# Weight sums of a Strassen step by accumulating DMAs inside SBUF, with the block products in another order

## The chip, the cores and the metric

The kernel runs on one core of one Trainium2 chip. The metric is device time in microseconds (us). The engines are PE (TensorE, matrix products), DVE (VectorE), ACT (ScalarE), POOL (GpSimd) and SP (SyncE, which here only issues DMAs). Each engine works through its own list of instructions in order and waits on semaphores for the others. SBUF is the on-chip memory, 128 partitions; PSUM holds the accumulators of matrix products.

## The reference

The kernel computes a trunk of four pre-norm layers over 256 tokens of width 1024, in fp32. Each layer is a mixer with a memory attention beside it, an output projection, and a dense SwiGLU FFN. The change lies in the FFN alone:

```python
def _swiglu(x, w_in, w_out):
    gu = x @ w_in
    return (jax.nn.silu(gu[..., :D_FF]) * gu[..., D_FF:]) @ w_out
```

`D_FF` is 2816, so `w_in` is 1024 x 5632 and `w_out` 2816 x 1024.

## The kernel before, in words

Weights come from HBM in chunks of 512 KB, [128, 2, 512] in fp32: SP issues the load (L124 in `wchunk`, L220 in `strassen`) into one of eight buffers of the pool `wraw`. A product in fp32 precision is made of three matmuls in the faster format fp32r. For that each chunk is split into a high and a low part in `wparts`: ACT casts `whi` (L131), DVE subtracts to get `wlo` (L132). There are eight buffers of `whi` and eight of `wlo`, so a cast waits until PE is through with the chunk eight places ahead. PE then runs hi x hi, hi x lo, lo x hi (L136 to L138; L214 to L216 in `strassen`).

An FFN has six blocks of hidden columns, b = 0 to 5. In blocks 1 and 4, and once in the middle of the output projection (`hidden_products`), a 2 x 2 block product [tokens] x [weights] is made with seven block products in place of eight (Strassen's scheme in Winograd's form). This is `strassen`; I call its three places in a layer A (b = 1), B (b = 4) and C (in the output projection). Four layers make twelve calls.

In such a call the weight quarters are b11, b12 (upper row), b21, b22 (lower row). Each is loaded in two halves of depth, s = 0 and 1, each one chunk of 512 KB. The numbers of the products and the weights that they take are:

| product | weight operand |
|---|---|
| 1 | b11 |
| 5 | t = b11 + b12 |
| 7 | b12 + b22, written over b12 |
| 6 | t + b22, written over t |
| 2 | b21 |
| 4 | t + b21, written over t again |
| 3 | b22 |

The tile t is `wsum` in the profile and sits in a `wraw` buffer too. I write 6_0 for the half of product 6 with s = 0. A half of a product is six matmuls of 128 x 512. Before the change all sums are made by DVE in `plus` (L224), four for each s: eight a call. Products add up in shared accumulators (`banks`): 1 and 2 in one, 5 and 3 in one, 7 and 4 in one, 6 in its own. Between them DVE reads accumulators out: u = acc6 + v, y = acc7 + u (L224), then `out` hands quarters of the result on (`gated`, L905 to L913 for A and B; `quarter`, L936 for C). So product 4 may start in the accumulator of 7 only when y has been read from it, and product 3 in that of 5 only when L911 (in C: L936) has read it.

The order on each engine is set by a scheduler from the order of the code and the dependencies; within an engine it is fixed. n0, n1, ... are the weight chunks that follow a call. `flush` runs work that was put off with `later`, such as the transposes of hidden columns (`hidden`, L890 to L894). In block 4 `hidden_side` makes the token sums that C needs out of such a transposed tile, `src`. `rstd` (L329, L330) and two small products for `lamt` (L694) are POOL's only work near the calls.

Of the kernel before, what the change touches and what calls it, by code (L numbers as in the profile page):

```python
# [13 lines left out]
ALU = mybir.AluOpType  # L14
# [3 lines left out]
P = 128  # L18
# [22 lines left out]
def trunk_kernel(ctx, tc, x, mem, vecs, w_in, w_kv, w_o, w_f1, w_f2, lams, g_final, out):  # L41
    nc = tc.nc
# [85 lines left out]
    def wparts(raw, nk=2, ncol=512):  # L128
        hi = wsplit.tile([P, nk, ncol], F32R, name="whi", tag="whi")
        lo = wsplit.tile([P, nk, ncol], F32R, name="wlo", tag="wlo")  # L130
        nc.scalar.copy(hi, raw)  # L131
        wlast[:] = [nc.vector.tensor_tensor(lo, raw, hi.bitcast(F32), ALU.subtract)]  # L132
        return hi, lo
# [12 lines left out]
    def flush():  # L146
        for item in pend:
            item[0] -= 1
        for item in [i for i in pend if i[0] <= 0]:
            pend.remove(item)  # L150
            item[1]()
# [45 lines left out]
    def strassen(left, right, ab, out):  # L197

        acc = {}
        banks = {1: 1, 2: 1, 5: 5, 3: 5, 7: 7, 4: 7, 6: 6}

        def product(p, w, s):
            b = banks[p]
            if b not in acc:
                acc[b] = ps_acc.tile([P, 512], F32, name="acc", tag="ps")
            lh, ll = ab[p]  # L210
            for k in range(2):
                kc = 2 * s + k
                start, stop = kc == 0 and p == b, kc == 3
                nc.tensor.matmul(acc[b], lh[:, kc, :], w[0][:, k, :], start=start, stop=False, skip_group_check=True)  # L214
                nc.tensor.matmul(acc[b], lh[:, kc, :], w[1][:, k, :], start=False, stop=False, skip_group_check=True)  # L215
                nc.tensor.matmul(acc[b], ll[:, kc, :], w[0][:, k, :], start=False, stop=stop, skip_group_check=True)  # L216

        def load(cols, r):
            raw = wraw.tile([P, 2, 512], F32, name="raw", tag="raw")
            nc.sync.dma_start(raw, cols[r:r + 2 * P, :].rearrange("(c p) n -> p c n", p=P))  # L220
            return raw

        def plus(out, a, b):
            nc.vector.tensor_tensor(out, a, b, ALU.add)  # L224

        part = lambda name: work.tile([P, 512], F32, name=name, tag="att", bufs=NATT)
        b22, sums = [], []
        v, u, y = part("sv"), part("su"), part("sy")
        for s in range(2):
            b11, b12 = (load(c, 2 * s * P) for c in (left, right))  # L230
            b22.append(load(right, 512 + 2 * s * P))
            product(1, wparts(b11), s)
            t = wraw.tile([P, 2, 512], F32, name="wsum", tag="raw")
            plus(t, b11, b12)
            if s == 1:
                nc.scalar.copy(v, acc[1])
            product(5, wparts(t), s)
            flush()
            plus(b12, b12, b22[s])
            product(7, wparts(b12), s)  # L240
            plus(t, t, b22[s])
            product(6, wparts(t), s)
            flush()
            sums.append(t)
        plus(u, acc[6], v)
        plus(y, acc[7], u)
        b21 = [load(left, 512 + 2 * s * P) for s in range(2)]
        for s in range(2):
            product(2, wparts(b21[s]), s)
        out(0, 0, acc[1], None)  # L250
        out(1, 1, acc[5], y)
        flush()
        for s in range(2):
            plus(sums[s], sums[s], b21[s])
            product(4, wparts(sums[s]), s)
            if s == 1:
                out(1, 0, acc[7], u)
            product(3, wparts(b22[s]), s)
            flush()
        out(0, 1, acc[5], u)  # L260

    def negative(rs):
        out = []
# [5 lines left out]
    def token_parts(src):  # L269
        hi = work.tile([P, 4, P], F32R, name="sh", tag="att", bufs=NATT)  # L270
        lo = work.tile([P, 4, P], F32R, name="sl", tag="att", bufs=NATT)
        nc.scalar.copy(hi, src)
        nc.vector.tensor_tensor(lo, src, hi.bitcast(F32), ALU.subtract)
        return hi, lo
# [432 lines left out]
    for i in range(DEPTH):  # L707
# [136 lines left out]
        hab, hsum = {}, {}  # L844

        def hidden_side(k, t, src):

            tt, stt = nc.vector.tensor_tensor, nc.vector.scalar_tensor_tensor
            if k == 0 and t == 0:
                both = big.tile([P, 2, 4, P], F32, name="hsum", tag="big")  # L850
                hsum["d"], hsum["a21"] = both[:, 0], both[:, 1]
                nc.scalar.copy(hsum["d"], src)
            elif k == 0:
                nc.scalar.copy(hsum["a21"], src)
                tt(hsum["d"], hsum["d"], src, ALU.subtract)
                hab[7] = token_parts(hsum["d"])
            elif t == 1:
                tt(hsum["a21"], src, hsum["a21"], ALU.subtract)
                hab[5] = token_parts(hsum["a21"])
                stt(hsum["d"], hsum["d"], -1.0, src, ALU.mult, ALU.subtract)  # L860
                hab[6] = token_parts(hsum["d"])
            else:
                stt(hsum["a21"], src, -1.0, hsum["d"], ALU.mult, ALU.subtract)
                hab[3] = token_parts(hsum["a21"])
                for p, g, t in ((1, 3, 0), (2, 4, 0), (4, 4, 1)):
                    hab[p] = tuple(x[:, :, t * P:(t + 1) * P] for x in hts[g])

        for b in range(6):
# [18 lines left out]
            def hidden(t, s, hh, hl, n, b):  # L887
                tr = ps_x.tile([P, 4, P], F32, name="tr", tag="ps")
                for c in range(n // P):
                    nc.tensor.transpose(tr[:, c, :], s[:, c * P:(c + 1) * P], ident)  # L890
                src = tr[:, :n // P, :]
                hi = hh[:, :, t * P:(t + 1) * P]
                nc.scalar.copy(hi, src)
                nc.vector.tensor_tensor(hl[:, :, t * P:(t + 1) * P], src, hi.bitcast(F32), ALU.subtract)  # L894
                if b in (3, 4):
                    hidden_side(b - 3, t, src)
# [3 lines left out]
            if b in (1, 4):  # L900
                def gated(t, side, ps, add, sg=sg, hh=hh, hl=hl, b=b, up={}):
                    if side == 0:
                        src = ps
                        if add is not None:
                            nc.vector.tensor_tensor(sg[t], ps, add, ALU.add)  # L905
                            src = sg[t]
                        nc.scalar.activation(sg[t], src, AF.Silu, scale=rx[t])
                        up[t, 0] = sg[t]
                    else:
                        up[t, 1] = add if t == 1 else work.tile([P, 512], F32, name="sx", tag="att", bufs=NATT)  # L910
                        nc.vector.tensor_tensor(up[t, 1], ps, add, ALU.add)  # L911
                    if (t, 0) in up and (t, 1) in up:
                        nc.vector.scalar_tensor_tensor(sg[t], up[t, 1], rneg[t], sg[t], ALU.mult, ALU.mult)  # L913
                        later(2, lambda: hidden(t, sg[t], hh, hl, 512, b))

                strassen(gcols, ucols, ab, gated)
            elif n == 512:
                proj([gcols], xT, lambda t, ps: h_out(t, ps, None))
                if b == 0:
                    ab, rneg = tokens_side(xg, xT), negative(rx)  # L920
                proj([ucols], xT, lambda t, ps: h_out(t, None, ps))
            else:
                proj([gcols, ucols], xT, lambda t, ps: h_out(t, ps[:, :n], ps[:, n:2 * n]))
# [14 lines left out]
        def hidden_products():  # L938
            w = w_f2[i, 12 * P:20 * P, :]
            strassen(w[:, :512], w[:, 512:], hab, quarter)  # L940
# [35 lines left out]
```

## Time and profile before

| what | value |
|---|---|
| median of three runs | 1271.62 us (1271.61 to 1271.62) |
| the profiled execution | 1271.41 us, span 1269.7 us |
| granted TensorE clock, mean | 0.999 |
| PE busy | 1258.3 us (99%) |
| DVE busy | 1022.4 us (81%) |
| ACT busy | 753.3 us (59%) |
| POOL busy | 55.7 us (4%) |
| bytes moved by DMA | 227.35 MB, mean 179 GB/s |

How to read it: a row of the groups gives line, engine, operation, output <- inputs, shape and count, then busy time in us and the mean of one in ns, then the idle time of the engine ahead of these instructions and what ended it. A row of the waits gives who waited for what: us in total, times, longest. A row of a timeline gives start and duration in us; matmuls are pipelined, so that their durations overlap and the distance of two starts tells the rate. A row of a stretch gives its length, busy time and count of each engine, the granted clock, the share of the DMA engines, and GB/s.

### The profile page before, as it was taken

To read this page: it belongs to the slowest core of one execution; us is meant where nothing else is said; L and a number is where in the kernel's file an instruction comes from. 1 tells how busy PE (TensorE), PEld (TensorE's weight loads), DVE (VectorE), ACT (ScalarE), POOL (GpSimd) and SP (SyncE) were. 2 spreads that over 40 slices of the span, in tenths; PEclk is the share of its full clock that TensorE was granted. 3 is DMA by queue.
4 is the path that set the end of the run, shared out by engine and by line. 5 is a ranking of instruction groups with operands and counts; after the bars stand their busy time and mean duration, and the time that the engine had idled before them with its cause. 6 is when DMAs were issued, how large, how long until landed. Compare 5 with 4: busy or idle time off the path is not lost.

```text
span 1269.7 us, 16380 instructions
## 1 busy us (share of the span) xinstructions
PE 1258.3 (99%) x6031; PEld 1036.9 (82%) x6031; DVE 1022.4 (81%) x1271; ACT 753.3 (59%) x1067; POOL 55.7 (4%) x109
## 2 busy tenths in 40 slices
PE   8999999999999999999999999999999999999997
PEld 6888888888888888888888888888888888888886
DVE  6765699899867669989986777989996646997995
ACT  7756466575555646656655545656556655674743
POOL 1000000000111000000000000000000001000001
PEclk9999999999999999999999999999999999999999
DMA  9644538366764444836575563665486444384561
GB/s 345 203 150 133 149 116 276 106 207 193 261 193 130 136 149 116 282 116 219 192 247 172 164 197 103 185 215 180 166 272 209 133 133 149 100 260 138 199 200 66
DMA packets 111888, 227.35 MB, mean 179 GB/s; under 512 B 7488, under 2 KB 20288, under 8 KB 111808
## 3 DMA queue, kind: packets, MB, share of 16 engines
q1 hardware_dynamic: 111808, 226.31, 55.6%
q8 instruction: 47, 0.77, 0.2%
q14 instruction: 33, 0.27, 0.1%
HBM read 225.23 MB, written 1.05 MB: 178 GB/s over the span
## 4 chain that ended last, share of the span: by engine, by line
PE 95%; DVE 2%; ACT 1%; issue 1%; DMA 0%; SPq 0%; POOL 0%; POOLq 0%; ACTq 0%
PE acc L136 23%; PE acc L138 23%; PE acc L137 23%; PE acc L214 6%; PE acc L216 6%; PE acc L215 6%; PE tr L890 2%; PE tr L363 1%; DVE wlo L132 1%; PE tr L349 1%; PE tr L432 1%; PE at L413 1%; PE at L445 1%; PE at L479 1%; PE at L521 1%; DVE wsum L224 1%
## 5 line engine op out<-in xcount | busy, mean ns | idle before, releaser
L132 DVE TENSOR_TENSOR wlo<-raw,whi 128x1024 fp32r<-128x1024 f32 (+1 forms) x428 | 508.0, 1210 | 101.3 <-ACT whi L131 99.0
L131 ACT CAST whi<-raw 128x1024 fp32r<-128x1024 f32 (+1 forms) x428 | 434.1, 1041 | 198.8 <-PE acc L138 122.6
L136 PE MATMUL acc<-whi,xth 128*128 128x512 f32 (+1 forms) x896 | 353.6, 395 | 1.1 <-ACT xth L356 1.1
L137 PE MATMUL acc<-wlo,xth 128*128 128x512 f32 (+1 forms) x896 | 342.9, 383 | 1.3 <-DVE wlo L132 1.3
L138 PE MATMUL acc<-whi,xtl 128*128 128x512 f32 (+1 forms) x896 | 343.9, 384 | 0.0
L138 PEld LDWEIGHTS acc<-whi,xtl 128*128 128x128 f32 x896 | 168.4, 188 | 33.8
L137 PEld LDWEIGHTS acc<-wlo,xth 128*128 128x128 f32 x896 | 168.9, 189 | 32.3 <-DVE wlo L132 2.5
L136 PEld LDWEIGHTS acc<-whi,xth 128*128 128x128 f32 x896 | 168.7, 188 | 32.5 <-ACT xth L356 1.6
L131 ACT CAST whi<-wsum 128x1024 fp32r<-128x1024 f32 x72 | 75.7, 1052 | 85.4 <-DVE wsum L224 81.5
L132 DVE TENSOR_TENSOR wlo<-wsum,whi 128x1024 fp32r<-128x1024 f32 x72 | 87.7, 1218 | 1.5 <-ACT whi L131 0.7
L214 PE MATMUL acc<-whi,sh 128*128 128x512 f32 x192 | 75.9, 396 | 0.0
L136 PE MATMUL acc<-whi,hh 128*128 128x512 f32 x192 | 75.6, 394 | 0.0
L216 PE MATMUL acc<-whi,sl 128*128 128x512 f32 x192 | 74.9, 390 | 0.0
L138 PE MATMUL acc<-whi,hl 128*128 128x512 f32 x192 | 74.8, 390 | 0.0
L215 PE MATMUL acc<-wlo,sh 128*128 128x512 f32 x192 | 74.8, 390 | 0.0
L137 PE MATMUL acc<-wlo,hh 128*128 128x512 f32 x192 | 74.8, 390 | 0.0
L224 DVE TENSOR_TENSOR wsum<-wsum,raw 128x1024 f32<-128x1024 f32 x48 | 57.8, 1218 | 0.3
L136 PE MATMUL acc<-whi,oh 128*128 128x512 f32 x128 | 51.1, 400 | 0.0
L138 PE MATMUL acc<-whi,ol 128*128 128x512 f32 x128 | 50.0, 391 | 0.0
L137 PE MATMUL acc<-wlo,oh 128*128 128x512 f32 x128 | 49.9, 390 | 0.0
L214 PEld LDWEIGHTS acc<-whi,sh 128*128 128x128 f32 x192 | 36.1, 188 | 8.2 <-DVE sy L911 1.1
L216 PEld LDWEIGHTS acc<-whi,sl 128*128 128x128 f32 x192 | 36.1, 188 | 7.7
(236 smaller groups left out, 1762.9 us busy)
## 6 DMA issues: line engine op xcount, KB each, us to landing
raw<-in_w_ffn_in SPq DMA_DIRECT2D x160, 512.0 KB, 4.5
raw<-in_w_in SPq DMA_DIRECT2D x100, 512.0 KB, 4.8
raw<-in_w_ffn_out SPq DMA_DIRECT2D x88, 512.0 KB, 4.4
raw<-in_w_o SPq DMA_DIRECT2D x40, 512.0 KB, 4.1
raw<-in_w_mem_kv SPq DMA_DIRECT2D x16, 512.0 KB, 4.4
raw<-in_w_ffn_in SPq DMA_DIRECT2D x32, 256.0 KB, 3.2
raw<-in_w_in SPq DMA_DIRECT2D x8, 256.0 KB, 5.6
x<-in_x SPq DMA_DIRECT2D x4, 256.0 KB, 3.9
```

What stands on the lines that cost most here:

```text
L131: nc.scalar.copy(hi, raw)
L132: wlast[:] = [nc.vector.tensor_tensor(lo, raw, hi.bitcast(F32), ALU.subtract)]
L136: nc.tensor.matmul(ps, lh, wh, start=first, stop=False)
L137: nc.tensor.matmul(ps, lh, wl, start=False, stop=False)
L138: return nc.tensor.matmul(ps, ll, wh, start=False, stop=last)
L214: nc.tensor.matmul(acc[b], lh[:, kc, :], w[0][:, k, :], start=start, stop=False, skip_group_check=True)
L215: nc.tensor.matmul(acc[b], lh[:, kc, :], w[1][:, k, :], start=False, stop=False, skip_group_check=True)
L216: nc.tensor.matmul(acc[b], ll[:, kc, :], w[0][:, k, :], start=False, stop=stop, skip_group_check=True)
L224: nc.vector.tensor_tensor(out, a, b, ALU.add)
L349: last_pe = nc.tensor.transpose(ps[:, c, :], src[:, kc * P:(kc + 1) * P], ident).ins
L363: nc.tensor.transpose(ps[:, c, :], src[:, c * P:(c + 1) * P], ident)
L890: nc.tensor.transpose(tr[:, c, :], s[:, c * P:(c + 1) * P], ident)
```

## The change

Of the eight sums of a call two stay on DVE (t = b11 + b12, for s = 0 and 1). The other six become DMAs that POOL issues (L228 of the changed kernel) and that add their source to their target, from SBUF to SBUF, 512 KB each. I number them D0 to D5 in the order in which POOL issues them in A:

- D0, D1: b12 += b22 for s = 0, 1, once t is formed
- D2, D3: t += b22, once product 5's split of t is made
- D4, D5: t += b21, once product 6's split of t is made

The products run 1, 5 (s = 0), 1, 5 (s = 1), then 7, 6, 2, 3, 4, each with both halves together. `out(0, 1)` comes ahead of `out(1, 0)`, and `hidden_side` takes the two token tiles of its second step in the other order. One `flush` of a call falls away. Other lines keep their work; behind L224 the numbers shift by 5 to 7 (L891 was L884, L901 was L894, L918 was L911).

```diff
+        def add_by_dma(out, a):
+            nc.gpsimd.dma_start(out, a, accum_op=ALU.add)
+
+        b12, b22, sums = [], [], []
         v, u, y = part("sv"), part("su"), part("sy")
         for s in range(2):
-            b11, b12 = (load(c, 2 * s * P) for c in (left, right))
+            b11 = load(left, 2 * s * P)
+            b12.append(load(right, 2 * s * P))
             b22.append(load(right, 512 + 2 * s * P))
             product(1, wparts(b11), s)
             t = wraw.tile([P, 2, 512], F32, name="wsum", tag="raw")
-            plus(t, b11, b12)
+            plus(t, b11, b12[s])
+            add_by_dma(b12[s], b22[s])
             if s == 1:
                 nc.scalar.copy(v, acc[1])
             product(5, wparts(t), s)
-            flush()
-            plus(b12, b12, b22[s])
-            product(7, wparts(b12), s)
-            plus(t, t, b22[s])
-            product(6, wparts(t), s)
+            add_by_dma(t, b22[s])
             flush()
             sums.append(t)
+        for s in range(2):
+            product(7, wparts(b12[s]), s)
+        b21 = [load(left, 512 + 2 * s * P) for s in range(2)]
+        flush()
+        for s in range(2):
+            product(6, wparts(sums[s]), s)
+            add_by_dma(sums[s], b21[s])
         plus(u, acc[6], v)
         plus(y, acc[7], u)
-        b21 = [load(left, 512 + 2 * s * P) for s in range(2)]
         for s in range(2):
             product(2, wparts(b21[s]), s)
         out(0, 0, acc[1], None)
         out(1, 1, acc[5], y)
         flush()
         for s in range(2):
-            plus(sums[s], sums[s], b21[s])
+            product(3, wparts(b22[s]), s)
+        out(0, 1, acc[5], u)
+        flush()
+        for s in range(2):
             product(4, wparts(sums[s]), s)
-            if s == 1:
-                out(1, 0, acc[7], u)
-            product(3, wparts(b22[s]), s)
-            flush()
-        out(0, 1, acc[5], u)
+        out(1, 0, acc[7], u)
...
-            elif t == 1:
+            elif t == 0:
+                hsum["a12"] = src
+            else:
                 tt(hsum["a21"], src, hsum["a21"], ALU.subtract)
                 hab[5] = token_parts(hsum["a21"])
                 stt(hsum["d"], hsum["d"], -1.0, src, ALU.mult, ALU.subtract)
                 hab[6] = token_parts(hsum["d"])
-            else:
-                stt(hsum["a21"], src, -1.0, hsum["d"], ALU.mult, ALU.subtract)
+                stt(hsum["a21"], hsum["a12"], -1.0, hsum["d"], ALU.mult, ALU.subtract)
```

The order on DVE at the start of type A in layer 0, before. wsum_1797 is t for s = 0, raw_1780 and raw_1782 are b11 and b12 for s = 0, raw_1841 is b11 for s = 1; the sum in the fifth row is t += b22.

```order
L132 TENSOR_TENSOR wlo_1787<-raw_1780,whi_1786 128x1024
L132 TENSOR_TENSOR wlo_1800<-wsum_1797,whi_1799 128x1024
L132 TENSOR_TENSOR wlo_1819<-raw_1782,whi_1818 128x1024
L273 TENSOR_TENSOR sl_1678<-xg_1514,sh_1677 128x512
L224 TENSOR_TENSOR wsum_1797<-wsum_1797,raw_1784 128x1024
L273 TENSOR_TENSOR sl_1683<-xg_1542,sh_1682 128x512
L884 SCALAR_TENSOR_TENSOR sg_1579<-acc_1714,rstd_1522,sg_1579 128x512
L132 TENSOR_TENSOR wlo_1831<-wsum_1797,whi_1830 128x1024
```

And the same place in the changed kernel, where wsum_1797 and wsum_1835 are t for s = 0 and 1, raw_1819 is b11 for s = 1, raw_1782 and raw_1821 are b12:

```order
L132 TENSOR_TENSOR wlo_1787<-raw_1780,whi_1786 128x1024
L132 TENSOR_TENSOR wlo_1801<-wsum_1797,whi_1800 128x1024
L132 TENSOR_TENSOR wlo_1826<-raw_1819,whi_1825 128x1024
L279 TENSOR_TENSOR sl_1678<-xg_1514,sh_1677 128x512
L132 TENSOR_TENSOR wlo_1840<-wsum_1835,whi_1839 128x1024
L279 TENSOR_TENSOR sl_1683<-xg_1542,sh_1682 128x512
L891 SCALAR_TENSOR_TENSOR sg_1579<-acc_1714,rstd_1522,sg_1579 128x512
L132 TENSOR_TENSOR wlo_1851<-raw_1782,whi_1850 128x1024
L132 TENSOR_TENSOR wlo_1862<-raw_1821,whi_1861 128x1024
L901 TENSOR_TENSOR hl_1578<-tr_1753,hh_1577 128x4x128
L132 TENSOR_TENSOR wlo_1876<-wsum_1797,whi_1875 128x1024
```

The splits of 1_1 and 5_1 have moved ahead of those of product 7, and no sum stands between them any more.

Later in the same call, where product 4's weights are split and y is read, on DVE before (wlo_1922 and wlo_1943 belong to 4_0 and 4_1, wlo_1932 to 3_0, su_1778 is u, sy_1779 is y):

```order
L132 TENSOR_TENSOR wlo_1922<-wsum_1797,whi_1921 128x1024
L132 TENSOR_TENSOR wlo_1932<-raw_1784,whi_1931 128x1024
L224 TENSOR_TENSOR wsum_1857<-wsum_1857,raw_1896 128x1024
L224 TENSOR_TENSOR su_1778<-acc_1834,sv_1777 128x512
L224 TENSOR_TENSOR sy_1779<-acc_1822,su_1778 128x512
L132 TENSOR_TENSOR wlo_1943<-wsum_1857,whi_1942 128x1024
L911 TENSOR_TENSOR sy_1779<-acc_1803,sy_1779 128x512
```

and in the changed kernel (wlo_1923 and wlo_1933 belong to 3_0 and 3_1, wlo_1946 and wlo_1956 to 4_0 and 4_1, wlo_1975, wlo_1981 and wlo_1987 to n0, n1 and n2):

```order
L132 TENSOR_TENSOR wlo_1923<-raw_1784,whi_1922 128x1024
L132 TENSOR_TENSOR wlo_1933<-raw_1823,whi_1932 128x1024
L132 TENSOR_TENSOR wlo_1946<-wsum_1797,whi_1945 128x1024
L132 TENSOR_TENSOR wlo_1956<-wsum_1835,whi_1955 128x1024
L132 TENSOR_TENSOR wlo_1975<-raw_1972,whi_1974 128x1024
L224 TENSOR_TENSOR su_1778<-acc_1879,sv_1777 128x512
L132 TENSOR_TENSOR wlo_1981<-raw_1978,whi_1980 128x1024
L224 TENSOR_TENSOR sy_1779<-acc_1854,su_1778 128x512
L132 TENSOR_TENSOR wlo_1987<-raw_1984,whi_1986 128x1024
L918 TENSOR_TENSOR sy_1779<-acc_1804,sy_1779 128x512
```

Now u and y stand behind both splits of product 4 and behind those of n0 and n1. On PE, type A starts four matmuls of n0 ahead of 4_0, then runs two of 4_1, then 3_0 and 3_1, and then the rest; B starts one matmul of n0 there; C runs 3_0, 3_1, 4_0, 4_1.

POOL's list in layer 0, changed (raw_1784 and raw_1823 are b22, raw_1871 and raw_1873 b21; the last row is B's D0):

```order
L228 DMA raw_1782<-raw_1784 128x1024
L335 TENSOR_SCALAR rstd_1522<-ss_1520 128x1
L336 TENSOR_TENSOR rstd_1522<-rstd_1522,nhalf_99 128x1
L335 TENSOR_SCALAR rstd_1574<-ss_1572 128x1
L336 TENSOR_TENSOR rstd_1574<-rstd_1574,nhalf_99 128x1
L228 DMA raw_1821<-raw_1823 128x1024
L228 DMA wsum_1797<-raw_1784 128x1024
L228 DMA wsum_1835<-raw_1823 128x1024
L228 DMA wsum_1797<-raw_1871 128x1024
L228 DMA wsum_1835<-raw_1873 128x1024
L228 DMA raw_2326<-raw_2328 128x1024
```

Between rstd and D1 nothing else stands; D0 has come ahead of the two pairs of rstd.

More of the change, by code (lines that the diff above doesn't have):

```diff
@@ L226, in strassen @@
         part = lambda name: work.tile([P, 512], F32, name=name, tag="att", bufs=NATT)
-        b22, sums = [], []
+        def add_by_dma(out, a):
+            nc.gpsimd.dma_start(out, a, accum_op=ALU.add)
+        b12, b22, sums = [], [], []
         v, u, y = part("sv"), part("su"), part("sy")
         for s in range(2):
-            b11, b12 = (load(c, 2 * s * P) for c in (left, right))
+            b11 = load(left, 2 * s * P)
+            b12.append(load(right, 2 * s * P))
             b22.append(load(right, 512 + 2 * s * P))
```

## The prediction, made before the changed kernel ran

> **What bounds the kernel now.** I read the page first: engine shares, the DMA line, the chain.
>
> ```profile
> PE 1258.3 (99%) x6031; PEld 1036.9 (82%) x6031; DVE 1022.4 (81%) x1271; ACT 753.3 (59%) x1067; POOL 55.7 (4%) x109
> ...
> DMA packets 111888, 227.35 MB, mean 179 GB/s; under 512 B 7488, under 2 KB 20288, under 8 KB 111808
> ...
> q1 hardware_dynamic: 111808, 226.31, 55.6%
> ...
> PE 95%; DVE 2%; ACT 1%; issue 1%; DMA 0%; SPq 0%; POOL 0%; POOLq 0%; ACTq 0%
> ```
>
> PE is the bound: busy for 99% of the span and 95% of the chain. DVE, from which the change takes work, is the second engine. Then the groups, for the size of that work, and the waits, for who stands behind it.
>
> ```profile
> L132 DVE TENSOR_TENSOR wlo<-raw,whi 128x1024 fp32r<-128x1024 f32 (+1 forms) x428 | 508.0, 1210 | 101.3 <-ACT whi L131 99.0
> ...
> L224 DVE TENSOR_TENSOR wsum<-wsum,raw 128x1024 f32<-128x1024 f32 x48 | 57.8, 1218 | 0.3
> L224 DVE TENSOR_TENSOR wsum<-raw 128x1024 f32<-128x1024 f32 x24 | 29.6, 1233 | 6.5 <-DMA raw<-in_w_ffn_in 6.4
> L224 DVE TENSOR_TENSOR raw<-raw 128x1024 f32<-128x1024 f32 x24 | 29.3, 1221 | 1.4 <-DMA raw<-in_w_ffn_in 0.8
> ```
>
> ```profile
> ACT whi L131 <- PE acc L138: 125.1, 124, 5.1
> ...
> ACT whi L131 <- DVE wsum L224: 81.5, 37, 4.9
> ...
> PEld acc L137 <- DVE wlo L132: 2.5, 3, 1.1
> PEld acc L214 <- DVE sy L224: 1.9, 7, 0.3
> ...
> PEld acc L214 <- DVE sy L911: 1.1, 4, 0.3
> ```
>
> ACT waits 81.5 us for weight sums, but PE hardly waits for what ACT and DVE make of them. In the block products (L214 to L216) its named waits are 1.9 us for y of L224 and 1.1 us for L911. Then I cut the span into the twelve stretches from the first to the last block product, in the order A, B, C of each layer.
>
> ```profile
> core 0: us, PE busy (x) PEld busy (x) DVE busy (x) ACT busy (x) POOL busy (x), PEclk, DMA share, GB/s
> 184.17:203.97 19.80, 19.80 (x90) 16.01 (x88) 19.77 (x22) 13.57 (x16) 0.00 (x0) 1.00 0.62 193
> 250.01:269.53 19.52, 19.52 (x90) 16.16 (x89) 19.39 (x21) 15.58 (x19) 0.00 (x0) 1.00 0.69 212
> 298.19:317.79 19.60, 19.38 (x86) 15.69 (x84) 19.60 (x22) 12.34 (x14) 0.00 (x0) 1.00 0.63 186
> 499.65:519.47 19.82, 19.82 (x90) 16.01 (x88) 19.79 (x22) 13.59 (x16) 0.00 (x0) 1.00 0.62 195
> ...
> 613.74:632.94 19.20, 19.20 (x86) 15.69 (x85) 19.16 (x21) 13.25 (x15) 0.00 (x0) 1.00 0.63 201
> ...
> 1221.69:1240.89 19.20, 19.20 (x86) 15.70 (x84) 19.16 (x21) 13.26 (x15) 0.00 (x0) 1.00 0.65 205
> ```
>
> DVE is full in all of them, and yet PE is too. What can PE still gain? The first stretch on PE:
>
> ```profile
> 184.17 0.39 PE L214 MATMUL acc<-whi,xth 128*128 128x512 f32 x1
> ...
> 186.89 0.60 PE L890 MATMUL tr<-ident,sg 128*128 128x128 f32 x4
> 187.25 0.48 PE L214 MATMUL acc<-whi,sh 128*128 128x512 f32 x1
> ...
> 195.52 0.39 PE L214 MATMUL acc<-whi,xth 128*128 128x512 f32 x1
> ```
>
> Twelve matmuls start between 184.17 and 186.89, one each 0.227 us; a product half of six takes 1.36 us, four transposes 0.36 us. The 84 matmuls need 19.04 us, with the transposes 19.40 (type C has none inside). So A stands 0.40 us over its need, B 0.12, C 0.56 in layer 0 and 0.16 in layers 1 and 3. With the stretches not shown, close to these, all twelve are some 3.2 us over; that is the most a change to DVE can return here. B and the later C, where little is late, show that 0.12 to 0.16 stays. Reachable are 4 x 0.28 for A and 0.4 for the first C: 1.5 us.
>
> **The change part by part.**
>
> *72 sums leave DVE.* 12 stretches x 6 x 1.22 us = 88 us of busy time (of the three L224 groups, 48 + 24 leave, 24 stay). It lay beside PE; the gain on the end is the 1.5 us above, not 88. DVE falls to 934 us.
>
> *The other order of products* is free on PE: the same 84 matmuls. Its flush and hidden_side moves shift transposes and casts of a few 0.6 us against a DVE with 7 us less work in each stretch; I count nothing. Were that cover gone, two 0.69 us operations in each C would show, 6 us in all.
>
> *72 accumulating DMAs.* No such DMA is in this trace. Its landing time, L, from issue to the waiter's release, decides everything. The loads are nearest:
>
> ```profile
> raw<-in_w_ffn_in SPq DMA_DIRECT2D x160, 512.0 KB, 4.5
> ...
> raw<-in_w_o SPq DMA_DIRECT2D x40, 512.0 KB, 4.1
> ...
> memn<-in_mem SPq DMA_DIRECT2D x2, 512.0 KB, 11.3
> ```
>
> Lower end 4.1 us, a plain load of as many bytes; upper end 11.3 us, the slowest one of that size. Between: the q1 row gives 226.31 MB, 432 loads of 512 KB, in 55.6% of 1269.7 us, so 1.64 us of all engines for each. An accumulate reads a second operand: 4.5 + 1.64 = 6.1 us; a little more for its queue, since 6 x 1.64 to 3.3 us come on top of stretches whose DMA share is 0.62 to 0.69 already. I take 6.3 us, nearest to the ffn_in loads because it runs beside them.
>
> The Trainium skill (DMA: Bandwidth & Descriptors, Anatomy of one DMA) fits a DMA issued from GpSimd as 2.0 us plus bytes over 436 GB/s, and says (Collectives: The Full Stack, The bandwidth ceiling) that an add reads two sources, which doubles the read traffic. An estimate from both pages is 2.0 + 2 x 1.2 = 4.4 us; by it no sum is late and the kernel gains 1.5 us. The loads' 4.1 to 4.5 us here, against 3.2 us from the same fit, speak for more.
>
> *When each is wanted*, walked through type A of layer 0 with DVE's rows of before:
>
> ```profile
> 173.77 1.22 DVE L132 TENSOR_TENSOR wlo<-raw,whi 128x1024 fp32r<-128x1024 f32 x1
> 174.90 1.22 DVE L132 TENSOR_TENSOR wlo<-wsum,whi 128x1024 fp32r<-128x1024 f32 x1
> 176.04 1.22 DVE L132 TENSOR_TENSOR wlo<-raw,whi 128x1024 fp32r<-128x1024 f32 x1
> 177.17 0.69 DVE L273 TENSOR_TENSOR sl<-xg,sh 128x512 fp32r<-128x512 f32 x1
> 177.78 1.23 DVE L224 TENSOR_TENSOR wsum<-wsum,raw 128x1024 f32<-128x1024 f32 x1
> 178.91 0.69 DVE L273 TENSOR_TENSOR sl<-xg,sh 128x512 fp32r<-128x512 f32 x1
> 179.51 0.75 DVE L884 SCALAR_TENSOR_TENSOR sg<-acc,rstd,sg 128x512 f32<-128x512 f32 x1
> ```
>
> In the new order DVE splits 1_0, 5_0, 1_1, then sl, then 5_1 in the place of the sum at 177.78. So D2 is issued when 5_0's split ends, 176.1, and D3 when 5_1's ends, 179.1. With eight split buffers the cast for a product half can start once the half eight places ahead has left PE: for 6_0 (the seventh) one chunk before 184.17, at 182.8, and for 6_1 at 184.2. D2 has 6.6 us, D3 5.1. A late D3 first only delays the cast of 6_1. 6_0's split ends about 185.2 and issues D4; 6_1's, after one more DVE operation, 187.05 and issues D5 (2.85 us after its cast could begin: cast 1.05, wait 0.6, split 1.2).
>
> D4 and D5 are wanted by the casts of 4_0 and 4_1. On ACT and DVE these stand ahead of the next chunks n0 and n1 and of y, and product 4 may not start on PE before y is read out of its accumulator. PE reaches 4_0 after 2_0, 2_1 and four matmuls of n0: 195.52 + 2.72 + 0.91 = 199.15. Behind 4_1's cast (1.05) DVE still has the splits of 4_1, n0, n1 (3 x 1.13 from row to row), u (0.6) and y (0.7) to do: the cast must begin at 193.2. D5 so has 6.15 us by itself, and through D3: 179.1 + L + 2.85 + L = 193.2, L = 5.6. Beyond that an A stretch stalls 2L - 11.25 us.
>
> In B the same splits come earlier against PE:
>
> ```profile
> 237.25 1.22 DVE L132 TENSOR_TENSOR wlo<-wsum,whi 128x1024 fp32r<-128x1024 f32 x1 [0.18 <-ACT whi L131]
> ```
>
> This is 5_0's, 11.5 us ahead of PE's 250.01, where A has 8.0. 5_1's follows some 3.5 us later, 8 us ahead. The same walk then gives D4 and D5 6.6 us, and the way through D3 a stall of 2L - 14.85, from 7.4. In C product 3 runs ahead of 4, and it takes 8.4 us. D0 and D1 have 10 us and more everywhere. The loads of two later chunks wait for D4 and D5 to free their buffers; landing 4.5 us on, they come no later than the y they stand behind.
>
> POOL issues the DMAs in order, and D0 stands ahead of the first rstd pair in layer 0:
>
> ```profile
> 156.74 0.19 POOL L329 TENSOR_SCALAR rstd<-ss 128x1 f32<-128x1 f32 x1 [21.93 <-ACT junk L336]
> ```
>
> ```profile
> 151.68 1.23 DVE L224 TENSOR_TENSOR wsum<-raw 128x1024 f32<-128x1024 f32 x1
> ```
>
> The sum at 151.68 is the last that D0 waits for (it reads b12_0 before D0 writes it), 3.8 us before rstd is due, so rstd is not held up. In C of layer 0 two products for lamt stand ahead of D1, which has 10 us.
>
> **Sum.** L = 6.3: A 4 x (12.6 - 11.25) = 5.4; B and C 0; less 1.5: +3.9 us. The profiled execution took 1271.41 us (span 1269.7), 0.2 under the median: 1275.3 against it, 1275.5 against the median. A difference of 0.2%, 2.5 us, is about what a measurement of this kernel tells from none.
>
> **Rivals.**
>
> Hidden. L up to 6.13: A stalls at most 1.0 each, 4.0 less 1.5 is +2.5. At L = 4.1 the result is -1.5: 1270.1. For it speaks that loads of the same size land in 4.1; against it the second operand.
>
> Faster by more than 2.5 us. DVE is full in the twelve stretches, and nearly all 3.2 us over would have to go: 1268.4 to 1269. Against it: 0.12 to 0.16 remain where nothing is late, and y and its successors keep their place on DVE.
>
> Late everywhere. If the accumulates and the 8 loads of a stretch queue behind each other, L = 8 gives A 4 x 4.75, B 4 x 1.4, less 1.5: +23, 1294.6. At 11.3: A 45, B 31, C some 16: +91, 1363.
>
> Starved. Were POOL held up in issuing while a DVE operation with two SBUF inputs runs, each DMA would wait for one such to end, up to 1.22 us, since DVE is full: L = 7.5, A 4 x 3.75, B 4 x 0.9, +17, 1289. POOL's only rows in the neighbourhood are small and show nothing of it.
>
> The Trainium skill (SBUF — State Buffer, SBUF: two separate sides, with its box on DVE blocking DMA) tells such a lock: descriptors that POOL writes are held back under some DVE copies. It adds under "Who interferes with whom" that tensor_tensor takes only the read side, by inference. No row of this trace has a DMA from POOL to test either.
>
> **How the numbers follow.** Late in A alone or a little in B (L 6.13 to 8): 0.42, and the forecast. Hidden: 0.40. Late everywhere or starved: 0.12. Faster: 0.06. So faster 0.06, same 0.40, slower 0.54. The range goes from 1269.4, the hidden case with a little more than the reachable gain, to 1295, L = 8; about 0.12 lies above and 0.05 below.
>
> **What would show it.** The DMA issues of the changed kernel give L directly. With L near 6.3 the four A stretches are 20.5 to 21 us long and PE waits there, at the first matmul of product 4 or of the chunk ahead of it, for y or wlo; ACT's casts of wsum wait for DMA instead of DVE; B and C stay within 0.2 us of before, the first C shorter by 0.4. DVE's busy time falls to 934 us with POOL's rows and the L224 group of 24 left. I am wrong if L is under 5.6 and A no shorter or longer, if stalls sit in the loads of later chunks, or if loads of 4.5 us grow so that the stretches behind the products lose time.

## The result and the profile after

| | before | changed |
|---|---|---|
| median, us | 1271.61 (1271.46 to 1271.62) | 1284.74 (1283.56 to 1287.49) |
| ratio to before | 1 | 1.0106, 95% interval 1.0091 to 1.0121 |
| profiled execution, us | 1271.41, span 1269.7 | 1283.56, span 1281.8 |

The change costs 13.1 us, 1.1%. From the page of the changed kernel: busy time, DMA queues, chain, DMA issues.

```profile
PE 1260.3 (98%) x6031; PEld 1036.0 (81%) x6031; DVE 943.5 (74%) x1199; ACT 759.5 (59%) x1067; POOL 117.8 (9%) x181
...
q1 hardware_dynamic: 111808, 226.31, 52.9%
q0 software_dynamic: 10368, 37.75, 16.2%
...
PE 77%; DMA 9%; DVE 6%; ACT 4%; issue 4%; POOL 1%; SPq 0%; POOLq 0%; ACTq 0%; DVEq 0%
...
raw<-raw POOLq DMA_DIRECT2D x24, 512.0 KB, 4.6
...
wsum<-raw POOLq DMA_DIRECT2D x48, 512.0 KB, 6.0
```

DVE lost 79 us of work as meant (1022.4 to 943.5), and the end came later. (The prediction's 88 us counts each sum at the 1.22 us of its row; in a full stretch rows follow each other at 1.13 us, which makes 72 sums 81 us.) The chain, 95% PE before, is now 77% PE and 9% DMA. The new queue q0 holds the accumulating DMAs: 16.2% of 1281.8 us over 72 is 2.88 us of all 16 engines for each, against 1.57 for a load (q1, 432 loads). D0 and D1 land in 4.6 us at the median, D2 to D5 in 6.0.

The same stretches from the first to the last block product: A, B and C of layer 0, then C of layer 1.

```profile
184.24:205.55 21.31, 20.73 (x93) 16.83 (x92) 19.05 (x19) 15.22 (x17) 1.71 (x2) 1.00 1.01 309
250.57:271.61 21.04, 20.35 (x90) 16.12 (x89) 19.96 (x21) 17.29 (x20) 1.74 (x2) 1.00 0.90 263
300.06:322.02 21.96, 19.30 (x86) 15.69 (x84) 17.52 (x19) 16.32 (x17) 1.71 (x2) 1.00 0.88 265
618.96:639.34 20.38, 19.32 (x86) 15.69 (x84) 17.55 (x19) 15.49 (x17) 1.73 (x2) 1.00 0.94 281
```

In A and C DVE is no longer full (19.05 and 17.52 us) and PE now is not either: in C it is busy 19.30 of 21.96 us. The DMA share, 0.62 to 0.69 before, is 0.88 and more. As A and B now hold some matmuls of the next chunk, lengths do not compare directly. So I took PE's stalls in the stretches from its timeline: of each distance between two starts that is over 0.25 us, what exceeds 0.2275 us (0.12 for a transpose). Sums in us over the four layers, one profiled execution each, with the kernels of the experiments (the rows of e7 and e11 also hold matmuls that ran at half the rate, see there):

| kernel | A | B | C layer 0 | C layers 1 to 3 | all | median, us |
|---|---|---|---|---|---|---|
| before | 1.2 | 0.4 | 0.5 | 0.4 | 2.5 | 1271.6 |
| changed | 3.7 | 3.2 | 2.9 | 4.8 | 14.5 | 1284.7 |
| e1 order only, sums on DVE | 4.0 | 0.5 | 0.1 | 0.0 | 4.6 | 1274.4 |
| e2 D0 to D3 by DMA | 2.6 | 0.4 | 6.4 | 16.0 | 25.4 | 1296.1 |
| e3 D0, D1, D4, D5 | 9.3 | 3.1 | 0.8 | 2.5 | 15.7 | 1286.2 |
| e4 D0, D1 | 3.9 | 0.5 | 2.6 | 6.4 | 13.4 | 1284.6 |
| e5 C on DVE | 2.9 | 2.8 | 0.0 | 0.0 | 5.7 | 1275.5 |
| e6 D0, D1 of C on DVE | 2.7 | 3.5 | 3.1 | 0.3 | 9.5 | 1279.3 |
| e7 old order, D4 and D5 | 21.4 | 11.7 | 4.7 | 15.7 | 53.5 | 1322.7 |
| e8 plain copies | 0.4 | 0.5 | 0.0 | 0.0 | 0.9 | 1269.8 |
| e9 halves | 7.2 | 0.4 | 2.9 | 2.0 | 12.4 | 1281.3 |
| e11 as e5, D4, D5 of B on DVE | 6.4 | 0.5 | 0.9 | 0.0 | 7.7 | 1276.0 |
| e12 as e6, lamt on DVE | 5.9 | 3.4 | 0.0 | 0.2 | 9.4 | 1277.6 |

Between before and changed the stalls grew by 12.0 us and the span by 12.1: the whole loss lies in these stretches, 2.4 in A, 2.8 in B, 6.8 in C.

The chain through A of layer 0 in the changed kernel, in order of time (start, length, what):

```profile
176.73 9.75 DMA wsum<-raw x2
...
187.64 1.24 DVE wlo L132
...
189.23 4.80 DMA wsum<-raw
...
194.12 1.06 ACT whi L131
...
196.35 1.22 DVE wlo L132
197.57 0.60 DVE su L224
...
199.22 0.69 DVE sy L224
...
199.96 0.50 PE acc L214
```

D2 and D3, the split of 6_1, D5, the cast of 4_1, the splits, u and y, product 4 on PE: the way that the prediction walked. C of layer 0:

```profile
290.00 13.93 DMA wsum<-raw x2
...
304.02 1.06 ACT whi L131
...
305.11 1.23 DVE wlo L132
...
306.75 6.43 DMA wsum<-raw
...
313.28 1.06 ACT whi L131
...
318.45 0.61 DVE sy L224
...
319.19 0.47 PE acc L214
```

The same links, but from the issue of D2 to the landing of D3 it takes 13.93 us here where it took 9.75 in A. POOL issues D3 4.5 us behind D2 here, with D1 between them, and 2.7 us behind it in A. D3 alone took 9.4, from the DMA issues of a stretch that holds only it; below it D1 of A of layer 0, which no other accumulate met:

```profile
wsum<-raw POOLq DMA_DIRECT2D x1, 512.0 KB, 9.4
```

```profile
raw<-raw POOLq DMA_DIRECT2D x1, 512.0 KB, 4.6
```

L, the landing time, which the prediction took as one number, runs from 4.5 us alone to 9.5 us behind two others.

### The profile page after: what moved, and what is told of

Read it like the earlier page. It is cut to its first block, busy times and chain, and to the rows that moved or that the text cites. A ratio compares the mean times of both kernels' runs of the same rounds, so it can differ in the third digit from the quotient of the medians.

```text
span 1281.8 us, 16653 instructions
## 1 busy us (share of the span) xinstructions
PE 1260.3 (98%) x6031; PEld 1036.0 (81%) x6031; DVE 943.5 (74%) x1199; ACT 759.5 (59%) x1067; POOL 117.8 (9%) x181
## 3 DMA queue, kind: packets, MB, share of 16 engines
q0 software_dynamic: 10368, 37.75, 16.2%
## 4 chain that ended last, share of the span: by engine, by line
PE 77%; DMA 9%; DVE 6%; ACT 4%; issue 4%; POOL 1%; SPq 0%; POOLq 0%; ACTq 0%; DVEq 0%
PE acc L136 19%; PE acc L138 19%; PE acc L137 19%; DMA wsum<-raw 8%; PE acc L214 3%; PE acc L216 3%; PE acc L215 3%; DVE wlo L132 3%; ACT whi L131 3%; PE tr L897 1%; PE tr L369 1%; PE tr L355 1%; PE tr L438 1%; PE at L419 1%; PE at L451 1%
## 5 line engine op out<-in xcount | busy, mean ns | idle before, releaser
L131 ACT CAST whi<-raw 128x1024 fp32r<-128x1024 f32 (+1 forms) x428 | 439.4, 1042 | 252.5 <-PE acc L138 125.0
L228 POOL DMA_DIRECT2D raw<-raw x24 | 21.3, 889 | 462.5 <-DVE wsum L224 155.7
L228 POOL DMA_DIRECT2D wsum<-raw x48 | 41.5, 865 | 202.9 <-DVE wlo L132 136.1
```

The costliest lines, as they stand in the source:

```text
L228: nc.gpsimd.dma_start(out, a, accum_op=ALU.add)
```

## The experiments

**First round: which sums cost it?** My first theory after the result was queueing: D3 and D5 stand behind other accumulates. The rivals were the new order by itself, and the volume of transfers. The edits of e1 to e4 put some of the sums back on DVE (the comments say in which kernel a line is changed):

```diff
-            add_by_dma(b12[s], b22[s])            # D0, D1: e1
+            plus(b12[s], b12[s], b22[s])
-            add_by_dma(t, b22[s])                 # D2, D3: e1, e3, e4
+            plus(t, t, b22[s])
-            add_by_dma(sums[s], b21[s])           # D4, D5: e1, e2, e4
+            plus(sums[s], sums[s], b21[s])
```

e1, the order alone. 

> The changed kernel with all eight sums back on DVE: the new order of products alone. Queue theory (the loss is PE waiting at product 4 because accumulates that stand behind one another land late, 6 to 9.5 us in place of 4.6): no accumulate, no loss, 1270 to 1273 us, PE stalls in the twelve stretches 2 to 4 us in all. Order theory (u and y stand behind the splits of product 4 and of the next chunks, so the order itself costs): most of the 13 us stay, 1280 to 1285. Volume theory (72 more transfers slow the weight loads, in proportion): as before, 1271.6.

e2. 

> D0 to D3 by DMA, D4 and D5 (t += b21) on DVE. Queue theory: D3 still lands late in type C (8 to 9 us), but nothing that is issued after it has to land before product 4, so the split of 6_1 still comes before PE needs it; 1271 to 1274 us. Order theory: 1280 to 1285. Volume theory: 48 of 72 accumulates leave two thirds of the loss, 1280.

e3. 

> D0, D1, D4, D5 by DMA, D2 and D3 (t += b22) on DVE. Queue theory: D1 and D4 have the queue almost to themselves (4.6 us), D5 stands behind D4 (6 to 7 us) and is issued some 2 us sooner than with a late D3; A and C lose little, B up to 1 us each as now: 1272 to 1277 us. Volume theory: 1280, as e2. Order theory: 1280 to 1285.

e4. 

> Only D0 and D1 (b12 += b22) by DMA, four sums on DVE. Queue theory: these two have 10 us and more and meet no other accumulate, so no loss and DVE has 29 us less to do: 1270 to 1272 us. Volume theory: a third of the loss, 1276. Order theory: 1280 to 1285.

Measured: e1 1274.38 us, ratio 1.0021 (1.0011 to 1.0030); e2 1296.05, 1.0188 (1.0173 to 1.0203); e3 1286.18, 1.0114 (1.0097 to 1.0131); e4 1284.59, 1.0101 (1.0086 to 1.0116). Each ratio here and below is to runs of the kernel before beside it: median 1271.67 us in this round, 1271.73 for e5 to e8, 1271.95 for e9 to e12.

Only e1 came near. The order theory falls as the main cause: alone the order costs 2.7 us, all of it in A. The volume theory falls: 24 DMAs (e4) cost as much as 72, and the 48 of e2 cost 11 us more than all. And the queueing theory falls as I had put it: e4, in which no accumulate of t exists, loses 13 us, 9.0 us of stalls in C. Its chain through C of layer 1 shows how:

```profile
604.55 0.23 PE tr L897 x2
...
604.81 0.38 ACT hb L900
...
605.21 0.42 DVE hb L901
605.64 2.27 DVE wlo L132 x2
607.90 1.15 DVE wsum L224
...
612.61 1.22 DVE wlo L132
613.83 1.15 DVE wsum L224
...
615.61 5.87 DMA raw<-raw
...
621.58 1.06 ACT whi L131
...
626.07 2.35 DVE wsum L224 x2
```

t = b11 + b12 is summed for s = 0 at 607.90 and for s = 1 at 613.83. Only then may D0 and D1 overwrite b12, and the split of 7_1 waits 5.87 us for D1. ACT and DVE work in order, so all behind it slides, and DVE, which has four more sums to do here, is full from there on. In the changed kernel only the second of the two comes late there (596.70 and 609.31). In C these sums come late because DVE does them behind the split of the last hidden columns (hb), which waits for PE's transposes. In A, D1 was issued at 171.79, 12 us ahead of PE's first product; in C of layer 0 of the changed kernel at 292.75, 7 us ahead.

e2's larger loss shows the same in its C of layer 1. There t is summed at 610.82 for s = 0 and at 615.48 for s = 1, both late, so D0 to D3 are all issued between 612.68 and 619.53 and land in 5.7 to 9.6 us. The cast of 7_1 waits 6.11 us for D1, and DVE stands idle for 5.94 us behind it:

```profile
625.61 1.05 ACT L131 CAST whi<-raw 128x1024 fp32r<-128x1024 f32 x1 [6.11 <-DMA raw<-raw]
```

After that the two sums t += b21, on DVE in e2, stand ahead of the split of 2_0, for which PE waits 1.9 us. So the costs of the DMAs do not add up: it matters what DVE has to do behind the late landing. I did not trace why A stalls 9.3 us in e3.

**Second round: take C away, take D0 and D1 of C away.** Before I had followed that chain to its start I put the lateness down to the loads of the second halves, and the expectations say so. Both kernels use one switch (the calls pass n = 0, 2 and 4 for D0 and D1, D2 and D3, D4 and D5):

```diff
-        def add_by_dma(out, a):
-            nc.gpsimd.dma_start(out, a, accum_op=ALU.add)
+        def add_by_dma(out, a, n):
+            if n in on_dve:
+                plus(out, out, a)
+            else:
+                nc.gpsimd.dma_start(out, a, accum_op=ALU.add)
...
-            strassen(w[:, :512], w[:, 512:], hab, quarter)
+            strassen(w[:, :512], w[:, 512:], hab, quarter, (0,))     # e5: (0, 2, 4)
```

e5. 

> The changed kernel, but in type C all eight sums on DVE; A and B keep their six DMAs. The queue theory as first put has fallen: with D0 and D1 alone the time was 1284.6 us, and its stalls lie in C. New theory, the late load: in C the second halves of the weights land just in time, since their buffers come free late, and D1 puts its 5 to 8 us between such a load and the split of 7_1, behind which ACT and DVE keep in order the splits of 6, 4 and y. Then the loss in C (7.7 us of PE stalls now, 0.1 with the order alone) goes, and A's and B's stay: 1276 to 1278 us. If transfers as such cost (volume), 48 of 72 remain: 1280.

e6. 

> As the changed kernel, but in type C D0 and D1 on DVE, D2 to D5 by DMA. Late load: D1 no longer stands between load and split, D2 and D3 meet one transfer less; most of C's 7.7 us go, 1276 to 1279 us. If in C it is D2 and D3 that come late by queueing, C keeps its loss: 1282 to 1285.

Measured: e5 1275.46 us, 1.0032 (1.0021 to 1.0043); e6 1279.29, 1.0066 (1.0049 to 1.0083). The loss in C is the DMAs': without them its stalls are 0.0. In layers 1 to 3 it hangs on D0 and D1 (4.8 to 0.3 us with these two on DVE). ACT in C of layer 1 of the changed kernel shows two waits, of 7_1's cast for D1 and of 6_1's cast for D3:

```profile
618.24 1.05 ACT L131 CAST whi<-raw 128x1024 fp32r<-128x1024 f32 x1 [5.61 <-DMA raw<-raw]
...
621.99 1.05 ACT L131 CAST whi<-wsum 128x1024 fp32r<-128x1024 f32 x1 [1.74 <-DMA wsum<-raw]
```

D1 landed 7.2 us after its issue, D3, issued behind D2 and D1, 8.5 us after; in e6 D3 landed in 6.2. The chain of the changed kernel goes through the landing of D3, not of D1. As e6 takes away both D1's own landing and its place ahead of D3, how the loss divides between the two is not shown. So the second half of the theory holds, that a landing stands between a late input and the split, with queueing as a part of it; the first does not: in e4's C of layer 1 the load of b12_1 was issued at 601.13 and took 3.5 us, so it lay ready 9 us before the sum. What is late is the sum on DVE. In layer 0 the 3.1 us stayed. POOL's timeline of e6 there:

```profile
290.51 1.51 POOL L703 TENSOR_TENSOR lamt<-lamt 128x128 f32<-128x128 f32 x1 [36.18 <-DMA lamt<-in_lams]
292.34 1.09 POOL L703 TENSOR_TENSOR lamt<-lamt 128x128 f32<-128x128 f32 x1 [0.31 <-DMA lamt<-in_lams]
293.37 0.88 POOL L231 DMA_DIRECT2D wsum<-raw  x1
```

```profile
289.35 1.22 DVE L132 TENSOR_TENSOR wlo<-wsum,whi 128x1024 fp32r<-128x1024 f32 x1
```

D2 could go when this split of 5_0 ended, at 290.57, but POOL issued it at 293.37, behind two small products that waited for their own loads. e12 moves those:

```diff
-            nc.gpsimd.tensor_tensor(lamt[:, j, :], lamt[:, 2 * j, :], lamt[:, 2 * j + 1, :], ALU.mult)
+            nc.vector.tensor_tensor(lamt[:, j, :], lamt[:, 2 * j, :], lamt[:, 2 * j + 1, :], ALU.mult)
```

> As e6 (in C only D0 and D1 on DVE), and the two lamt products of layer 0 on DVE instead of POOL. In e6 the C of layer 0 alone kept 3.05 us of stalls, against 0 to 0.2 in the other layers, and POOL issued its D2 4 us after the split that it waits for, behind the lamt products that waited for their loads. If that is the cause, this C falls to 0.5 or less and the time by 2.5 us, to 1276 to 1277. If it is the lamt loads ahead of the weight loads in SP's order, it stays at 1279.

Measured: 1277.56 us, 1.0046 (1.0032 to 1.0060), and this C has no stall left (3.1 to 0.0). The rival, the loads of lamt ahead of those of the weights, falls: SP's list is the same in e6 and e12. POOL's order was the cause there.

**B.** e11 is e5 with D4 and D5 of B on DVE as well:

```diff
-                strassen(gcols, ucols, ab, gated)
+                strassen(gcols, ucols, ab, gated, (4,) if b == 4 else ())
```

> As e5 (C on DVE), and in B also D4 and D5 on DVE. If B's loss (0.2 to 1.3 us a call) is D5 queueing behind D4, issued 1.8 us after it, B falls to 0.1 to 0.2 and the time to 1273 to 1274 us. If it is D2 and D3 or the order, it stays at 1275.5.

Measured: 1275.98 us, 1.0032 (1.0022 to 1.0041). By time a miss. B's stalls did fall as expected, 2.8 to 0.5 us, so they were D4's and D5's (in the changed kernel's B of layer 0 these landed in 6.5 and 7.1 us, issued 1.8 us apart). But A had 6.4 us in this profile, 4.2 of them in one call (layer 2). There the granted clock fell to 0.50 for a while after PE had waited for y:

```profile
822.00:824.00 2.00, 2.00 (x6) 1.52 (x5) 2.00 (x3) 0.00 (x0) 0.00 (x0) 0.50 1.05 388
```

Seven distances of 0.43 us in place of 0.23 make 1.4 of the 4.2 us; the rest are waits for y and for the split of n0. Among the five kernels that make all six sums of A by DMA in the same order, A's stalls are 2.7 to 6.4 us; what else moves them from run to run stays open.

**Is it the accumulate, or any DMA between two splits?** e8 leaves the additions out and copies as many bytes on the same queue, with every engine's list as in the changed kernel:

```diff
-            nc.gpsimd.dma_start(out, a, accum_op=ALU.add)
+            nc.gpsimd.dma_start(out, a)
```

> The changed kernel with 72 plain copies from SBUF to SBUF in place of the accumulating DMAs: the six sums of a call are left out, each target gets its source's bytes. If the second read is what makes them long (2.9 us of all engines each against 1.6 for a load), they land in 3.5 to 4 us alone and hardly queue: C loses 2 to 4, A only what the order costs, 2.7; 1275 to 1279 us. If the fixed latency between load and split is what costs, most of the loss stays: 1281 to 1284.

Measured: 1269.77 us, 0.9984 (0.9974 to 0.9993): faster than before by 2.0 us, and by 15 us than with additions. Its queue:

```profile
q0 software_dynamic: 10368, 37.75, 7.5%
...
wsum<-raw POOLq DMA_DIRECT2D x48, 512.0 KB, 3.8
```

7.5% of 1267.9 us over 72 is 1.32 us of engine time for a copy, against 2.88 for an accumulate: 2.2 times. Alone it lands in 3.0 us (D1 of A) against 4.6. With that the twelve stretches have 0.9 us of stalls in all, fewer than before. So the order is good, and DVE without the sums does return time; what takes it back is how long an accumulate takes. I had expected 1275 to 1279: 1.6 us less alone becomes much more where landings follow one another and queue.

e9 makes the accumulate smaller instead, with the other half of each sum on DVE:

```diff
-            nc.gpsimd.dma_start(out, a, accum_op=ALU.add)
+            nc.gpsimd.dma_start(out[:, 0, :], a[:, 0, :], accum_op=ALU.add)
+            plus(out[:, 1, :], out[:, 1, :], a[:, 1, :])
```

> The changed kernel with each of its 72 sums cut in two: the first 512 of a partition's 1024 numbers are added by DMA (256 KB), the others by DVE beside it. The plain copies showed that with 1.3 us of engine time in place of 2.9 a call has no stall at all (1269.8 us). An accumulate of half the bytes should need 1.4 us and land in some 3.2 us alone; DVE is rid of half of the 88 us. If engine time is what makes the sums late: A between 0.1 and 0.9 each, B and C near nothing, 1270 to 1273 us. If it is the accumulate as such, by a latency that does not shrink with the bytes, C and B keep half or more of their loss: 1277 to 1280.

Measured: 1281.30 us, 1.0071 (1.0058 to 1.0083). Half a miss. D1 of A lands in 3.4 us, near the expected 3.2, and B is clean (0.4), but A is worse (7.2) and C keeps 4.9. In A, DVE's halves stand ahead of the split of 5_1, so D3 is issued at 182.49 in place of 179.42; DVE then waits for 6_1's cast and is full from there on:

```profile
188.47 1.23 DVE L132 TENSOR_TENSOR wlo<-wsum,whi 128x1024 fp32r<-128x1024 f32 x1 [1.31 <-ACT whi L131]
189.61 1.29 DVE L224 TENSOR_TENSOR wsum<-wsum,raw 128x512 f32<-128x512 f32 x2
```

In C of layer 0, D0 stands behind the lamt products (issued at 291.76); C of layer 3 keeps 1.8 us that I did not trace.

**Looking for a version that beats both.** e7 takes the old order and only D4 and D5:

```diff
         b21 = [load(left, 512 + 2 * s * P) for s in range(2)]
+        for s in range(2):
+            nc.gpsimd.dma_start(sums[s], b21[s], accum_op=ALU.add)
...
-            plus(sums[s], sums[s], b21[s])
```

> The kernel before with its order of products, and only t += b21 made by DMA (24 of them, two a call), in the place of two sums on DVE that stand in the last third of a call. The loads of b21 are there early, t is free once 6's split is made; 4_0's weights have some 10 us, 4_1's some 5.8 us in A. Late load and queueing both give no stall at 4.6 us alone and DVE has two sums less where PE waits for y: 1270 to 1272 us. If 4_1's comes late in A, 1273 to 1276.

Measured: 1322.70 us, 1.0402 (1.0386 to 1.0417), the worst of all. In A of layer 0 D5 is issued when 6_1's split ends, and 4_1's cast waits for it:

```profile
191.12 0.88 POOL L249 DMA_DIRECT2D wsum<-raw  x1 [8.19 <-DVE wlo L132]
```

```profile
197.06 1.05 ACT L131 CAST whi<-wsum 128x1024 fp32r<-128x1024 f32 x1 [3.22 <-DMA wsum<-raw]
```

The landing, 5.9 us, is near the 5.8 us of slack that I had given 4_1. What I missed is that the scheduler now put u and y behind 4_1's split on DVE (before, they stood ahead of it), so that 4_0, too, waits for 4_1's sum. Besides, the granted clock, 1.00 around the calls of the changed kernel, fell to 0.50 for 3.4 or 6.8 us in eight of the twelve calls, first in this one:

```profile
204.00:207.00 3.00, 3.00 (x8) 2.31 (x7) 2.84 (x3) 1.04 (x1) 0.00 (x0) 0.50 0.95 327
```

Matmuls at half the rate make some 14 of the 53.5 us in the table. Each time it fell in or right behind a stall of PE, but what sets it off is not shown: a stall of 2.8 us in C of layer 0 of the changed kernel left the clock at 1.00.

e10 has no DMA sums, the old order in A and B, the new one in C (a copy of the changed `strassen` with all its sums by `plus`, called by `hidden_products`). 

> No DMA sums. A and B in the order of the kernel before, C in the changed order, all sums on DVE. From the stalls of the parts: A 0.3 each and B 0.1 as before, C 0 to 0.1 (order alone) in place of 0.5 and 0.1: 0.9 us less than before, 1270.5 to 1271. If the orders do not add, 1271.6.

Measured: 1271.26 us, 0.9995 (0.9986 to 1.0004): not told from before. Its stalls in A and B are those of before (1.3 and 0.4). No kernel here that computes the reference is clearly faster than before.

## Why the prediction was right or wrong

Forecast 1275.5 us in 1269.4 to 1295, slower with 0.54; measured 1284.74. The direction and the mechanism of A were right; the loss was three times the forecast's, and most of it came from places that I had costed at nothing. That 1284.7 lies in the range is partly luck: the range reached so far up for a queue that would delay A and B, with nothing in C, and C brought 6.8 of the 12.0 us.

- *The bound.* Right. PE is the bound, and all that DVE loses is worth little: e8 takes 2.0 us off, where I gave 1.5 as reachable and 3.2 as the most.
- *L = 6.3 us.* Right as a mean for D2 to D5 (6.0; 4.6 for D0 and D1), but by luck, and wrong as a single number. It was a load's 4.5 us plus 1.64 for a second read, and 0.2 for the queue. An accumulate by itself landed in 4.5 to 4.6 us at its quickest (D1 of A; the slowest that met no other accumulate took 6.0), no later than a load; the second read belonged on top of a copy's 3.0. The rest of the way to 6.0, and to 9.5, came with other transfers under way. To that the sum gave 0.2 us, though its own terms, 6 x 1.64 to 3.3 us in a stretch of 19.6 us, add 0.5 to 1.0 to a DMA share of 0.62 to 0.69. The estimate from the Trainium skill (4.4 us, DMA: Bandwidth & Descriptors, Anatomy of one DMA, with Collectives: The Full Stack, The bandwidth ceiling) is near those 4.5 to 4.6; the sum by it, a gain, failed because landings stand behind each other and behind late sums.
- *A, 5.4 us of stalls.* The chain is the one that I walked, link by link, with D3 issued at 179.42 (179.1 said) and D5 at 189.23. Their landings, 7.1 and 4.8 us, add up to 11.9 where the sum had 2L = 12.6. (The 193.2 for 4_1's cast is 193.4 by its own terms.) The stalls of A are 3.7, 2.4 more than before (forecast 4.3 more). What I had not seen: the order with sums on DVE costs A as much (e1: 4.0), because DVE is then too full for y to be early.
- *B, nothing below L = 6.6.* Failed on L and on the way taken. D5 stands behind D4 and took 7.1 us in layer 0; B has 2.8 us of stalls more than before, gone with these two on DVE (e11). But PE does not wait for y at product 4 there, as I had walked it. It waits already at 2_0, for v, the copy of product 1 (L241), which has to be made before product 2 adds to the same accumulator: ACT makes it behind the cast of 4_1, which waits for D5.

```profile
261.19 1.05 ACT L131 CAST whi<-wsum 128x1024 fp32r<-128x1024 f32 x1 [0.91 <-DMA wsum<-raw]
262.14 0.58 ACT L241 COPY sv<-acc 128x512 f32<-128x512 f32 x1
```

```profile
262.77 0.50 PE L214 MATMUL acc<-whi,xth 128*128 128x512 f32 x1 [0.69 <-ACT sv L241]
```

- *C, "it takes 8.4 us", and "D0 and D1 have 10 us and more everywhere".* This is the step that failed most, 6.8 us. I had walked D0 and D1 only in A, where loads come early. In C the sum t that D1 has to wait for comes late on DVE, behind work that waits for PE's transposes, and D1 puts its landing between that sum and the split of 7_1 (e4, e6); D3, which queues behind D1, then holds up 6_1. The gain of 0.4 us for the first C was lost with it.
- *POOL in order: "two products for lamt stand ahead of D1, which has 10 us".* Wrong for the same reason: D1 was issued 1.1 us behind the sum that it waits for. Under e6, where the products stand ahead of D2, that C kept 3.1 us, under e12 none.
- *Rivals.* "Late everywhere" is what happened in C. "Starved" did not: POOL's own time for an issue, with DVE busy 74% of the span, is 850 to 885 ns for 64 of the 72. The other eight, D0 and D1 of A, take 895 to 1068, at most 0.2 us more, where this rival had up to 1.22:

```profile
L228 POOL DMA_DIRECT2D wsum<-raw x48: 850/862/885, 176.7 to 1238.7; - x48
L228 POOL DMA_DIRECT2D raw<-raw x24: 852/870/1068, 153.6 to 1223.9; - x24
```

These are minimum, median and maximum in ns. The lock that the Trainium skill tells of (SBUF — State Buffer, in its box on DVE blocking DMA) does not show beside the tensor_tensor operations of this kernel, as its "Who interferes with whom" infers.

## What to carry to other kernels

Moving work from a busy engine to DMA trades throughput, which may have been free, for latency in a chain: price the landing in each place where the operation stands, first of all where its own input has only just been made, and add up landings that follow one another or share a queue. Behind a late landing every engine that works in order waits with all it has queued, so look at what the scheduler puts behind the first instruction that needs it. A copy in place of the accumulate told in one run that the time of the accumulate, not the new order nor the number of transfers, took the gain back.

## What the runs showed of the hardware that I had not expected

An accumulating DMA of 512 KB inside SBUF took 2.88 us of all 16 engines, a copy of the same bytes on the same queue 1.32: 2.2 times. One of 256 KB needed 1.53 us (8.6% of 1279.8 us over 72) and landed in 3.4 us alone, later than a 512 KB copy (3.0). POOL takes longer to issue one too: 862 ns against 530 for the copy, in the same rows of e8:

```profile
L228 POOL DMA_DIRECT2D wsum<-raw x48: 530/530/544, 176.7 to 1222.9; - x48
```
